# A two-layer perceptron by fast matrix products: more output buffers in chunk two, writes of x moved, and the first weight sums moved from GpSimd to VectorE and cut in halves

## The chip, the cores and the metric

The kernel runs on one core of a Trainium2 chip. TensorE (PE) multiplies matrices into PSUM (eight banks), VectorE (DVE) and ScalarE (ACT) read PSUM and SBUF, GpSimd (POOL) works on SBUF and issues transfers, SyncE (SP) only issues transfers. Each engine takes its own instructions in order, and semaphores tie them together. The metric is the time of one execution on the device in microseconds (us); lower is better. Several executions are timed, and one more is run under the hardware profiler.

## The reference

```python
batch, m, k, h, n = 16, 512, 768, 3072, 768      # x, w1, b1, w2 in float32
y = np.maximum(np.matmul(x, w1) + b1, 0)
return np.matmul(y, w2).astype(np.float32)
```

So 8192 rows of x go through a layer of 3072 hidden units and back to 768 columns.

## The kernel before, in words

Rows and hidden units are tiled so that both layers can be done with fewer products than blocks. Eight blocks of 1024 rows times two halves ("chunks") of the hidden units make 16 iterations: iterations 0 to 7 are chunk one, 8 to 15 chunk two. `NSB` is 8, `NIT` 16. Chunk one writes its output rows to DRAM, chunk two adds to them with accumulating transfers.

**First products (L475 to L589).** An iteration takes its rows of x as a 2 by 2 scheme of blocks, and each of its six strips of w1 (`TP` = 6) likewise. Iteration 0 uses plain products (`first_plain`, eight block products per strip, 24 matmuls of 512 columns). From iteration 1 on, `first` uses seven products per strip instead of eight, of 3 matmuls each, on sums of blocks: sums of x (`sums_x`, L383, slots `XS1`, `XS2`, `XS4` of the tile `x`) and sums of w1 (`sums_w1`, L281, slots `T1` to `T4` of a strip; `T3` takes the place of `B12`). ScalarE and VectorE turn the PSUM results into y; `s` is a scratch tile in SBUF with six slots, which first and second products share.

**Second products (L592 to L641).** y and w2 are combined in 20 products instead of the plain scheme's larger number, from sums of blocks of y (`sums_y`, L456, eight per pair of strips, on VectorE) and of w2 (`sum_w2`, L324, 16 sums, 15 of them on VectorE, the last one a negation on ScalarE). The list `SECOND` says for each of the 20 steps which product runs, into which pair of PSUM banks (q0 to q3), and which copies and sums follow it on ScalarE and VectorE. Eight of these are outputs o0 to o7, each 128 by 768 floats, made in the order o2, o3, o0, o5, o7, o4, o1, o6. Each takes a tile from a pool of four (L615) and is sent to DRAM at once: by SyncE in chunk one (L631), by GpSimd with accumulation in chunk two (L633).

**Order.** The program is written out by hand. `run` (L677) sorts the steps of all iterations by a key, so that the first strip of an iteration overlaps the last steps of the second products before it. After each step it pops one or two waiting sums of y (`fill`) and then runs the hooks that `plan` (L735) put behind it. A hook is named by kind, iteration, strip and step: `p1` plain first products, `m1` first products, `m2` second products. A step's place in this order is its place in the in-order stream of whichever engine or queue it uses, so an instruction that must wait holds up all that stands behind it on its engine.

What the diff touches:

- The loads at the start (L681 to L690) all stand in GpSimd's queue: strips of w1, twelve pieces of w2 (three for each of four slices s), rows of x.
- The sums of w1 for iteration 0 are hooks (L752 to L755): three for each strip after its first products, the fourth after step 4 of the second products, all 24 on GpSimd. The same function makes the sums for chunk two ahead of time (`ahead_w1`, L288).
- The sums of w2 for iteration 0 (L756 to L761) each take a whole block of 1536 columns: eight while strip 4 runs, one in strip 5, seven within the second products. Those for chunk two (L798 to L807) run at the end of iteration 7 and in iteration 8, from blocks fetched to the side into tiles of the pool `raw` and into x (`fetch_w2_aside`, L314).
- The second of the three sums of x (L392) runs on GpSimd.
- `save_x` (L400) writes x and its sums to DRAM for chunk two, in two parts, on SyncE's queue; for iterations 1 to 7 both are hooked behind step 16 of the second products before (L774, L775). `fetch_x` (L406) reads them back (L777, L779, L784).
- The pool `raw` has two buffers, for rows of x in chunk one and for w2 fetched aside in iterations 7 and 8.

Of the kernel before, what the change touches and what calls it, by code (L numbers as in the profile page):

```python
# [9 lines left out]
FP32 = mybir.dt.float32  # L10
# [3 lines left out]
ALU = mybir.AluOpType  # L14
# [135 lines left out]
class Fast:  # L150
# [127 lines left out]
                out=w[:, 2 * half:2 * half + 2].rearrange("p a k h -> p (a k) h"),  # L278
                in_=w1r[:, :, h0:h0 + P])

    def sums_w1(self, w, which=(0, 1, 2, 3)):  # L281
        every = ((self.T1, self.B12, self.B11), (self.T2, self.B22, self.T1),
                 (self.T4, self.B21, self.T2), (self.T3, self.B12, self.B22))
        for o, i, j in [every[n] for n in which]:
            self.nc.gpsimd.tensor_tensor(out=w[:, o], in0=w[:, i], in1=w[:, j],  # L285
                                         op=ALU.subtract)

    def ahead_w1(self, it, t, step):  # L288


        x0 = 4 * (it % 2)
        w = self.x[:, x0:x0 + 4].rearrange("p a k m -> p (a k m)")[:, 0:7 * 3 * P]
        w = w.rearrange("p (a k h) -> p a k h", a=7, k=3)
        if step == 0:
            self.load_strip(w, 1, t)
        elif step == 1:
            self.sums_w1(w)
        else:
            self.nc.sync.dma_start(out=self.w1dram[t], in_=w)

# [20 lines left out]
        self.nc.sync.dma_start(out=w, in_=self.w2dram[:, 2 * q:2 * q + 2])  # L321
        self.w2_raw[2 * q], self.w2_raw[2 * q + 1] = w[:, 0], w[:, 1]

    def sum_w2(self, n):  # L324

        o, i, j, sign = SUMS_W[n]

        def block(slot):
            return self.w2_raw.get(slot, self.v[:, slot].rearrange("p s n -> p (s n)"))

        out = self.v[:, o].rearrange("p s n -> p (s n)")
        if i is None:
            self.nc.scalar.activation(out=out, in_=block(j), func=ACTF.Copy,
                                      scale=float(sign))
        else:
            self.nc.vector.tensor_tensor(out=out, in0=block(i), in1=block(j),  # L336
                                         op=ALU.add if sign > 0 else ALU.subtract)
# [45 lines left out]
    def sums_x(self, it, which):  # L383

        x = self.x.rearrange("p a k m -> p a (k m)")
        a11 = 4 * (it % 2)
        a12, a21, a22 = a11 + 1, a11 + 2, a11 + 3
        if which == 0:
            self.nc.vector.tensor_tensor(out=x[:, self.XS1], in0=x[:, a21], in1=x[:, a22],  # L389
                                         op=ALU.add)  # L390
        elif which == 1:
            self.nc.gpsimd.tensor_tensor(  # L392
                out=x[:, a21:self.XS2 + 1:self.XS2 - a21],
                in0=x[:, a21:self.XS1 + 1:self.XS1 - a21],
                in1=x[:, a11:a11 + 1].to_broadcast((P, 2, 3 * self.MH)), op=ALU.subtract)
        else:
            self.nc.vector.tensor_tensor(out=x[:, self.XS4], in0=x[:, a12],
                                         in1=x[:, self.XS2], op=ALU.subtract)
# [193 lines left out]
    def second(self, it):  # L592
# [14 lines left out]
        def at(name):  # L607
# [2 lines left out]
                return self.ps[:, 2 * q:2 * q + 2, 0:NH]  # L610
            return self.s[:, int(name[1])].rearrange("p (a n) -> p a n", a=2)

        def total(engine, to, q, sign, kept=None, kept_sign=None):
            ps = at(f"q{q}")
            o = self.o_pool.tile([P, 2, NH], FP32, name="o") if to[0] == "o" else at(to)  # L615
            if kept is None:
                if engine == "ACT":
                    nc.scalar.activation(out=o, in_=ps, func=ACTF.Copy, scale=float(sign))  # L618
                else:
                    nc.vector.tensor_scalar(out=o, in0=ps, scalar1=float(sign), scalar2=None,  # L620
                                            op0=ALU.mult)
            else:
                a, b = (ps, at(kept)) if sign > 0 else (at(kept), ps)
                nc.vector.tensor_tensor(out=o, in0=a, in1=b,  # L624
                                        op=ALU.add if sign == kept_sign else ALU.subtract)
            if to[0] == "o":
                r, n = divmod(int(to[1]), 2)
                rows = self.of[row0 + r * QM:row0 + (r + 1) * QM, n * NH:(n + 1) * NH]
                rows = rows.rearrange("(j p) n -> p j n", p=P)
                if it < self.NSB:  # L630
                    nc.sync.dma_start(out=rows, in_=o)  # L631
                else:
                    nc.gpsimd.dma_start(out=rows, in_=o, accum_op=ALU.add)  # L633
# [43 lines left out]
    def run(self):  # L677
# [4 lines left out]
        self.constants()  # L682
        self.load_w1(1)
        self.load_x(0, (1,))
        for t in range(2, TP):
            self.load_w1(t)
        for s in range(4):
            for q in range(3):
                self.load_w2(self.v[:, 2 * q:2 * q + 2], 0, q, s)
        self.load_x(1, (0,))  # L690
# [44 lines left out]
    def plan(self):  # L735

        TP, NSB, NIT = self.TP, self.NSB, self.NIT
        self.hooks = {}

        def put(kind, it, q, i, fn, *args):  # L740
            self.hooks.setdefault((kind, it, q, i), []).append(lambda: fn(*args))
# [7 lines left out]
        put("p1", 0, 4, 1, self.transpose_x, 1, 0)  # L749
        put("p1", 0, 5, 1, self.transpose_x, 1, 1)  # L750
        put("m2", 0, 0, 3, self.save_x, 0, 0)
        for t in range(TP):  # L752
            put("p1", 0, max(t, 2), 3, lambda t: self.sums_w1(self.w1s[t], (0, 1, 2)), t)
        for t in range(TP):
            put("m2", 0, 0, 4, lambda t: self.sums_w1(self.w1s[t], (3,)), t)  # L755
        for n in range(8):  # L756
            put("p1", 0, 4, n // 2, self.sum_w2, n)
        for n, at in ((9, ("p1", 0, 5, 2)), (8, ("m2", 0, 0, 2)), (12, ("m2", 0, 0, 4)),
                      (10, ("m2", 0, 0, 5)), (14, ("m2", 0, 0, 7)), (13, ("m2", 0, 0, 9)),
                      (11, ("m2", 0, 0, 11)), (15, ("m2", 0, 0, 12))):  # L760
            put(*at, self.sum_w2, n)  # L761

        for it in range(NIT):
            nxt = it + 1
            if nxt < NSB:
# [5 lines left out]
                if nxt + 1 < NSB:  # L771
                    put("m2", it, 0, 5, self.load_x, nxt + 1, (0,))
                    put("m2", it, 0, 9, self.load_x, nxt + 1, (1,))
                put("m2", it, 0, 16, self.save_x, nxt, 0)  # L774
                put("m2", it, 0, 16, self.save_x, nxt, 1)  # L775
            elif nxt == NSB + 1:
                put("m2", it, 0, 8, self.fetch_x, nxt, 0)  # L777
            elif nxt < NIT:
                put("m1", it, 0, 4, self.fetch_x, nxt, 0)  # L779
            if nxt <= NSB:  # L780
                for n, i in enumerate((6, 7, 14)):
                    put("m2", it, 0, i, self.sums_x, nxt, n)
# [16 lines left out]
        put("m2", last, 0, 13, self.fetch_w2, B2)  # L799
        for n, at in ((2, ("m2", last, 0, 12)), (6, ("m2", last, 0, 14)),  # L800
                      (1, ("m2", last, 0, 16)), (15, ("m2", last, 0, 17)),
                      (3, ("m1", NSB, 0, 3)), (9, ("m1", NSB, 1, 1)), (7, ("m1", NSB, 1, 2)),
                      (0, ("m1", NSB, 1, 3)), (8, ("m1", NSB, 2, 1)), (5, ("m1", NSB, 2, 3)),
                      (12, ("m1", NSB, 3, 1)), (10, ("m2", NSB, 0, 5)),
                      (14, ("m2", NSB, 0, 6)), (4, ("m2", NSB, 0, 7)),
                      (13, ("m2", NSB, 0, 11)), (11, ("m2", NSB, 0, 14))):
            put(*at, self.sum_w2, n)  # L807

# [60 lines left out]
```

## Time and profile before

| What | us |
|---|---|
| Median of three runs | 933.2 (929.87 to 934.0) |
| Profiled execution, its own time | 931.92 |
| Span of that execution on the core | 930.4 |
| TensorE busy with matmuls | 875.0 (94%) |
| VectorE busy | 630.7 (68%) |
| ScalarE busy | 519.0 (56%) |
| GpSimd busy | 224.8 (24%) |

The page of the profile gives the busy time of each engine, then groups of instructions by line of the kernel: engine, operation, output and input by the program's names, shapes, how many, busy time, mean duration, and the idle time just before them with what ended it. `PEld` is the weight load of TensorE. The timeline has rows of start, length, engine, line and operation, several like instructions in a row merged (x8), with the idle time before them and its releaser in square brackets. Durations of instructions that follow one another closely overlap a little in the record, so the pitch in a row is shorter than a single duration.

### The profile page before, as it was taken

Reading aid. Unit: us, or ns where it says so; the run is one execution under the profiler, and the core shown is the slowest. Engines: PE = TensorE matmul, PEld = TensorE weight load, DVE = VectorE, ACT = ScalarE, POOL = GpSimd, SP = SyncE. Lnnn points to the kernel's source line nnn. Section 1 sums busy time; section 2 is a strip of 40 time slices with the busy share of each in tenths; the row PEclk is TensorE's granted clock in tenths of the full one; section 3 lists DMA queues with packets and bytes.
Section 4 is the critical chain, followed back from the end, with each engine's and each line's share of the span. In section 5 each row is a group of like instructions: output and inputs, shape, how many; then the busy total and the mean of one; then the engine's idle time right before and its main releaser. Section 6 shows DMA issues by size and latency. Waiting matters only on the chain.

```text
span 930.4 us, 12569 instructions
## 1 busy us (share of the span) xinstructions
PE 875.0 (94%) x4677; PEld 459.9 (49%) x4677; DVE 630.7 (68%) x1041; ACT 519.0 (56%) x791; POOL 224.8 (24%) x198
## 2 busy tenths in 40 slices
PE   8948999999999999999999899999999999999993
PEld 5424454554545555454545445455454545545452
DVE  2798676857767686776798656675766668566663
ACT  4723676757767576676346386675626345262530
POOL 6863042150503214040200301203030130402113
PEclk9978999999999999999999999999999999999997
DMA  9938849698687869818631925639173573815518
GB/s 201 199 110 162 254 86 309 87 248 209 133 283 108 294 86 265 173 70 343 270 119 51 228 45 153 102 119 136 36 156 64 145 110 119 122 19 101 83 18 120
DMA packets 120325, 138.11 MB, mean 148 GB/s; under 512 B 67116, under 2 KB 113732, under 8 KB 116420
## 3 DMA queue, kind: packets, MB, share of 16 engines
q0 software_dynamic: 50672, 46.41, 35.1%
q1 hardware_dynamic: 69264, 90.06, 29.7%
q10 hardware_dynamic: 324, 0.80, 0.3%
q8 instruction: 38, 0.62, 0.3%
q14 instruction: 27, 0.22, 0.1%
HBM read 72.17 MB, written 77.66 MB: 161 GB/s over the span
## 4 chain that ended last, share of the span: by engine, by line
PE 42%; issue 36%; DVE 8%; POOL 7%; DMA 4%; ACT 2%; POOLq 0%; DVEq 0%; ACTq 0%
PE ps L534 22%; PE ps L602 18%; POOL out_dram L633 7%; DMA out_dram<-o 4%; DVE o L624 2%; DVE v L336 2%; DVE y L466 2%; DVE ps L624 1%; DMA w1s<-in_w_dram 1%; PE ps L484 1%; ACT s L618 1%; ACT s L542 0%; ACT scrap L380 0%; ACT y L489 0%; DVE x L439 0%
## 5 line engine op out<-in xcount | busy, mean ns | idle before, releaser
L602 PE MATMUL ps<-v,y 128*128 128x384 f16 x2560 | 430.6, 329 | 17.3 <-DVE v L336 7.5
L534 PE MATMUL ps<-x,w1s 128*128 128x512 f16 x1890 | 417.0, 379 | 20.3 <-ACT s L542 14.2
L602 PEld LDWEIGHTS <-y 128*128 128x128 f16 x2560 | 251.4, 99 | 193.6 <-issue 11.0
L534 PEld LDWEIGHTS <-w1s 128*128 128x128 f16 x1890 | 184.9, 98 | 241.6 <-issue 25.2
L466 DVE TENSOR_TENSOR y<-y 128x512 f16<-128x512 f16 x512 | 212.0, 440 | 41.7 <-ACT y L551 26.3
L542 ACT ACTIVATE s<-ps,b1y 128x512 f32<-128x512 f32 x210 | 141.6, 687 | 172.1 <-PE ps L534 61.0
L546 DVE CUSTOM_DVE_ANT_0 y<-ps,s 128x512 f16<-128x512 f32 x210 | 144.9, 690 | 106.2 <-PE ps L534 73.6
L633 POOL DMA_DIRECT2D out_dram<-o x64 | 77.4, 1250 | 380.5 <-DVE o L624 378.5
L618 ACT ACTIVATE s<-ps 128x768 f32<-128x768 f32 x96 | 77.7, 810 | 133.4 <-PE ps L602 105.9
L624 DVE TENSOR_TENSOR o<-s,ps 128x768 f32<-128x768 f32 x64 | 61.0, 953 | 65.5 <-PE ps L602 22.7
L624 DVE TENSOR_TENSOR s<-ps,s 128x768 f32<-128x768 f32 x96 | 90.2, 953 | 12.6 <-ACT s L618 6.5
L624 DVE TENSOR_TENSOR o<-ps,s 128x768 f32<-128x768 f32 x64 | 59.3, 954 | 46.2 <-ACT s L618 36.4
L551 ACT ACTIVATE y<-ps,b1y 128x512 f16<-128x512 f32 x90 | 61.9, 687 | 39.7 <-PE ps L534 39.7
L392 POOL TENSOR_TENSOR x<-x 128x3072 f16<-128x3072 f16 x8 | 48.0, 6004 | 71.4 <-DVE x L389 71.4
L380 ACT ACTIVATE scrap<-xn 128x768 f16<-128x768 f16 x60 | 50.3, 838 | 0.8
L277 POOL DMA_DIRECT2D x<-in_w_dram x12 | 10.1, 848 | 163.7 <-PE ps L534 163.7
L557 ACT ACTIVATE ps<-ps,b1y 128x512 f32<-128x512 f32 x60 | 39.6, 659 | 10.8 <-PE ps L534 7.9
L551 ACT ACTIVATE y<-ps 128x512 f16<-128x512 f32 x60 | 35.8, 597 | 0.0
L344 ACT ACTIVATE scrap<-scrap 128x1536 f16<-128x1536 f16 x24 | 35.4, 1476 | 0.1
L618 ACT ACTIVATE ps<-ps 128x768 f32<-128x768 f32 x32 | 25.5, 798 | 9.8 <-PE ps L602 9.8
L484 PE MATMUL ps<-x,w1s 128*128 128x512 f16 x132 | 28.8, 379 | 0.4 <-DVE x L439 0.2
L285 POOL TENSOR_TENSOR w1s<-w1s 128x384 f16<-128x384 f16 x24 | 28.4, 1200 | 1.0
(64 smaller groups left out, 271.2 us busy)
## 6 DMA issues: line engine op xcount, KB each, us to landing
out_dram<-o SPq DMA_DIRECT2D x64, 384.0 KB, 5.2
out_dram<-o POOLq DMA_DIRECT2D x64, 384.0 KB, 6.3
xd<-x SPq DMA_DIRECT2D x8, 1536.0 KB, 6.5
x<-xd SPq DMA_DIRECT2D x8, 1536.0 KB, 8.2
xn<-in_x_dram POOLq DMA_DIRECT2D x15, 768.0 KB, 7.2
xd<-x SPq DMA_DIRECT2D x7, 1152.0 KB, 8.8
x<-xd SPq DMA_DIRECT2D x7, 1152.0 KB, 5.3
w1d<-x SPq DMA_DIRECT2D x6, 672.0 KB, 10.8
```

The lines of the kernel that those rows point to most:

```text
L380: self.nc.scalar.activation(out=self.junk(self.K), in_=rows, func=ACTF.Square, accum_out=self.stat[:, i:i + 1])
L392: self.nc.gpsimd.tensor_tensor(out=x[:, a21:self.XS2 + 1:self.XS2 - a21], in0=x[:, a21:self.XS1 + 1:self.XS1 - a21], in1=x[:, a11:a11 + 1] ...
L466: self.nc.vector.tensor_tensor(out=pair(*outs), in0=pair(*ins0), in1=pair(*ins1), op=ALU.add if sign > 0 else ALU.subtract)
L534: nc.tensor.matmul(ps, lhsT=w[:, slot, k, :], rhs=x[:, xslot, k, :], start=(start and k == 0), stop=(k == 2), skip_group_check=True)
L542: nc.scalar.activation(out=kept(name), in_=ps, func=ACTF.Identity, bias=bias)
L546: nc.vector._custom_dve(TENSOR_ADD_SAT, out=self.y_of(self.TP * half + t, m), in0=self.two(ps), in1=self.two(kept(name)), s0=F_MAX, s1=0.0)
L551: nc.scalar.activation(out=self.y_of(self.TP * half + t, m), in_=self.two(ps), func=ACTF.Relu, **kw)
L557: nc.scalar.activation(out=g["b"], in_=g["a"], func=ACTF.Identity, bias=bias1)
L602: nc.tensor.matmul(self.ps[:, 2 * q + j, 0:NH], lhsT=self.y[:, U_OF[p], m0:m0 + P], rhs=self.v[:, V_OF[p], s, :], start=(start and s == 0) ...
L618: nc.scalar.activation(out=o, in_=ps, func=ACTF.Copy, scale=float(sign))
L624: nc.vector.tensor_tensor(out=o, in0=a, in1=b, op=ALU.add if sign == kept_sign else ALU.subtract)
L633: nc.gpsimd.dma_start(out=rows, in_=o, accum_op=ALU.add)
```

## The change

Four things change.

- In chunk two from iteration 9 on, the outputs o5 and o7 share one tile from the pool `raw`, half each, and so do o1 and o6. The pool of four is left to o2, o3, o0 and o4.
- The two DRAM writes of x and its sums move from step 16 of the second products into the first products of the next iteration, the sums behind step 0 of strip 1 and x behind step 0 of strip 4. Fetches of x in chunk two move to other places too.
- In iteration 0 the 24 sums of w1 run on VectorE; three per strip come within the first products, the fourth one strip at a time in steps 8 to 13 of the second products. The sums of w2 are made as two halves each (slices 0 and 1, then 2 and 3), the first halves during strips 2 and 3, the second halves from strip 4 on, five of them within the second products. The loads of w1 strips and of w2 slices alternate. The second sum of x for iteration 1 also goes to VectorE.
- Some sums of w2 for chunk two move: sums 9 and 7 to steps 17 and 18 of iteration 7's second products, sum 4 from iteration 8's second products to its first. Sums 10 and 14 there read block B2 from its own slot instead of the copy aside.

```diff
-    def sums_w1(self, w, which=(0, 1, 2, 3)):
+    def sums_w1(self, w, engine, which=(0, 1, 2, 3)):
...
-            self.nc.gpsimd.tensor_tensor(out=w[:, o], in0=w[:, i], in1=w[:, j],
-                                         op=ALU.subtract)
+            engine.tensor_tensor(out=w[:, o], in0=w[:, i], in1=w[:, j], op=ALU.subtract)
...
-    def sum_w2(self, n):
+    def sum_w2(self, n, s0=0, s1=4):
 
         o, i, j, sign = SUMS_W[n]
 
-        def block(slot):
-            return self.w2_raw.get(slot, self.v[:, slot].rearrange("p s n -> p (s n)"))
-
-        out = self.v[:, o].rearrange("p s n -> p (s n)")
+        def block(slot, raw=self.w2_raw):
+            w = raw.get(slot, self.v[:, slot].rearrange("p s n -> p (s n)"))
+            return w[:, s0 * self.NH:s1 * self.NH]
+
+        out = block(o, {})
+        if self.w2_raw and o in (V6, V14):
+            self.w2_raw.pop(B2, None)
...
-            self.nc.gpsimd.tensor_tensor(
+            (self.nc.gpsimd if it > 1 else self.nc.vector).tensor_tensor(
...
+        pairs = {}
+
+        def output(to):
+
+            pair = {"o5": 0, "o7": 0, "o1": 1, "o6": 1}.get(to)
+            if it <= self.NSB or pair is None:
+                return self.o_pool.tile([P, 2, NH], FP32, name="o")
+            if pair not in pairs:
+                pairs[pair] = [self.raw_pool.tile([P, 4, NH], FP32, name="o2", tag="raw"), 0]
+            half = pairs[pair][1]
+            pairs[pair][1] = 2
+            return pairs[pair][0][:, half:half + 2]
+
...
-            o = self.o_pool.tile([P, 2, NH], FP32, name="o") if to[0] == "o" else at(to)
+            o = output(to) if to[0] == "o" else at(to)
...
-        for t in range(2, TP):
-            self.load_w1(t)
         for s in range(4):
+            self.load_w1(2 + s)
             for q in range(3):
                 self.load_w2(self.v[:, 2 * q:2 * q + 2], 0, q, s)
...
+        for t, at in enumerate(((1, 1), (1, 2), (2, 0), (2, 2), (3, 1), (4, 0))):
+            put("p1", 0, *at, lambda t: self.sums_w1(self.w1s[t], vector, (0, 1, 2)), t)
         for t in range(TP):
-            put("p1", 0, max(t, 2), 3, lambda t: self.sums_w1(self.w1s[t], (0, 1, 2)), t)
-        for t in range(TP):
-            put("m2", 0, 0, 4, lambda t: self.sums_w1(self.w1s[t], (3,)), t)
-        for n in range(8):
-            put("p1", 0, 4, n // 2, self.sum_w2, n)
-        for n, at in ((9, ("p1", 0, 5, 2)), (8, ("m2", 0, 0, 2)), (12, ("m2", 0, 0, 4)),
-                      (10, ("m2", 0, 0, 5)), (14, ("m2", 0, 0, 7)), (13, ("m2", 0, 0, 9)),
-                      (11, ("m2", 0, 0, 11)), (15, ("m2", 0, 0, 12))):
-            put(*at, self.sum_w2, n)
+            put("m2", 0, 0, 8 + t, lambda t: self.sums_w1(self.w1s[t], vector, (3,)), t)
+        for n in range(15):
+            put("p1", 0, 2 + n // 8, n % 8 // 2, self.sum_w2, n, 0, 2)
+            late = {10: 3, 12: 4, 14: 5, 13: 6, 11: 7}.get(n)
+            at = ("m2", 0, 0, late) if late else ("p1", 0, 4 + (n + 2) // 8, (n + 2) % 8 // 2)
+            put(*at, self.sum_w2, n, 2, 4)
+        put("m2", 0, 0, 12, self.sum_w2, 15)
...
-                put("m2", it, 0, 16, self.save_x, nxt, 0)
-                put("m2", it, 0, 16, self.save_x, nxt, 1)
-            elif nxt == NSB + 1:
-                put("m2", it, 0, 8, self.fetch_x, nxt, 0)
+                put("m1", nxt, 1, 0, self.save_x, nxt, 1)
+                put("m1", nxt, 4, 0, self.save_x, nxt, 0)
             elif nxt < NIT:
-                put("m1", it, 0, 4, self.fetch_x, nxt, 0)
+                put("m1", it, 4 if nxt == NSB + 1 else 2, 4, self.fetch_x, nxt, 0)
...
-                      (3, ("m1", NSB, 0, 3)), (9, ("m1", NSB, 1, 1)), (7, ("m1", NSB, 1, 2)),
-                      (0, ("m1", NSB, 1, 3)), (8, ("m1", NSB, 2, 1)), (5, ("m1", NSB, 2, 3)),
-                      (12, ("m1", NSB, 3, 1)), (10, ("m2", NSB, 0, 5)),
-                      (14, ("m2", NSB, 0, 6)), (4, ("m2", NSB, 0, 7)),
+                      (9, ("m2", last, 0, 17)), (7, ("m2", last, 0, 18)),
+                      (3, ("m1", NSB, 0, 3)), (0, ("m1", NSB, 1, 1)), (8, ("m1", NSB, 1, 2)),
+                      (4, ("m1", NSB, 1, 3)), (5, ("m1", NSB, 2, 1)), (12, ("m1", NSB, 2, 3)),
+                      (10, ("m2", NSB, 0, 5)), (14, ("m2", NSB, 0, 6)),
```

More of the change, by code (lines that the diff above doesn't have):

```diff
@@ L296, in ahead_w1 @@
         elif step == 1:
-            self.sums_w1(w)
+            self.sums_w1(w, self.nc.gpsimd)
         else:
@@ L738, in plan @@
         self.hooks = {}
+        vector = self.nc.vector
         def put(kind, it, q, i, fn, *args):
```

## The prediction

> **What bounds the kernel now.** I read the busy table first, then the stages side by side (one stage per iteration, cut where its last product begins), then the timeline of TensorE for its gaps, then VectorE and GpSimd around each gap.
>
> ```profile
> span 930.4 us, 12569 instructions
> PE 875.0 (94%) x4677; PEld 459.9 (49%) x4677; DVE 630.7 (68%) x1041; ACT 519.0 (56%) x791; POOL 224.8 (24%) x198
> ...
> 44.14:94.37 50.23, 33.18 (x164) 17.76 (x165) 46.65 (x46) 16.05 (x27) 26.68 (x20) 0.80 0.63 147
> ...
> 366.04:419.61 53.57, 53.38 (x288) 27.92 (x286) 37.48 (x64) 35.65 (x56) 11.26 (x7) 1.00 0.61 160
> ```
>
> TensorE is the bound: an undisturbed iteration (366.04 to 419.61) takes 53.57 us and TensorE works through all but 0.2 of it. (After the stretch and its length a stage's row has the busy time of TensorE, its weight loads, VectorE, ScalarE and GpSimd, then clock, DMA share and GB/s.) So only time in which it waits can be won, and that lies in four places. The first is the second half of iteration 0 (second row): 33.18 us of work in 50.23 us, at a granted clock of 0.80.
>
> ```profile
> 418.47 1.30 PE ps L602 x8
> 419.77 25.25 PE ps L534 x117
> ...
> 18.08 26.06 PE L484 MATMUL ps<-x,w1s 128*128 128x512 f16 x120 [0.24 <-DVE x L439]
> 53.08 4.15 PE L602 MATMUL ps<-v,y 128*128 128x384 f16 x14 [6.95 <-DVE v L336]
> 63.20 15.26 PE L602 MATMUL ps<-v,y 128*128 128x384 f16 x82 [5.97 <-DVE y L466]
> 82.07 10.51 PE L602 MATMUL ps<-v,y 128*128 128x384 f16 x48 [3.61 <-DVE o L624]
> ```
>
> At full speed eight matmuls of L602 take 1.30 us (0.162 each) and one of L534 25.25/117 = 0.216. That stretch holds 160 of the one and 3 of the other, so 26.6 us where 50.2 pass: 23.6 lost, 16.5 of it as the three gaps of the last rows, before which VectorE is late, the rest as small waits and slower matmuls behind them. VectorE is late because of GpSimd:
>
> ```profile
> L285 POOL TENSOR_TENSOR w1s<-w1s 128x384 f16<-128x384 f16 x24 | 28.4, 1200 | 1.0
> L466 DVE TENSOR_TENSOR y<-y 128x512 f16<-128x512 f16 x15 | 16.2, 1112 | 2.6 <-ACT y L489 2.4
> ...
> L466 DVE TENSOR_TENSOR y<-y x4: 410/411/413, 62.4 to 63.4; 128x512 f16<-128x512 f16 x4
> 510.92 1.82 DVE L336 TENSOR_TENSOR v<-w2r,x 128x1536 f16<-128x1536 f16 x2
> 74.17 6.99 DVE L336 TENSOR_TENSOR v<-v 128x1536 f16<-128x1536 f16 x2
> ```
>
> The first two rows are groups between 32.3 and 60.9 us, while GpSimd makes its 24 sums of w1: a sum of y takes 1.11 us. Just after, the same sum takes 0.41. Two sums of w2 alone take 1.82 together (0.95 each, 0.87 apart); beside GpSimd's 6 us sum of x (last row) two take 6.99.
>
> The other places are the ends of iterations:
>
> ```profile
> 151.49 22.82 PE L534 MATMUL ps<-x,w1s 128*128 128x512 f16 x105 [0.80 <-DMA out_dram<-o]
> 206.10 22.82 PE L534 MATMUL ps<-x,w1s 128*128 128x512 f16 x105 [0.89 <-ACT s L542]
> 261.49 22.82 PE L534 MATMUL ps<-x,w1s 128*128 128x512 f16 x105 [1.66 <-ACT s L542]
> 528.72 0.81 PE L534 MATMUL ps<-x,w1s 128*128 128x512 f16 x3 [2.99 <-DVE o L624]
> 535.92 22.82 PE L534 MATMUL ps<-x,w1s 128*128 128x512 f16 x105 [2.50 <-ACT s L542]
> ...
> L534 PE MATMUL ps<-x,w1s 128*128 128x512 f16 x879 | 194.1, 379 | 11.6 <-ACT s L542 11.6
> ```
>
> The last row is the group of L534 from 531 us to the end: 11.6 us of waits for ScalarE, so 9.1 beside the 2.50 at 535.92, one wait at the end of each of iterations 9 to 14 (1.5 each).
>
> **The change, part by part.**
>
> *w1 and w2 sums of iteration 0.* GpSimd loses all 24 sums and one 6 us sum of x. VectorE gains them: a 384-wide sum by the slope between 512 (0.41) and 1536 (0.95) is 0.34 alone, 0.27 in a row; the sum of x, twice 1536, 1.7; and w2 comes as halves of 768, 0.55 alone, 0.47 in a row. From 24.0 us (strip 1 ends at 18.08+24x0.217 = 23.3, ScalarE needs 0.7) VectorE has until the end of first products: 24 sums of y at 0.36 (0.41 alone, overlapping), 12 of w1 at 0.27, 25 halves at 0.47: 8.6+3.2+11.8 = 23.6, so it ends at about 48, TensorE at 44.1. Data is there:
>
> ```profile
> 22.88 2.81 DVE L466 TENSOR_TENSOR y<-y 128x512 f16<-128x512 f16 x7 [4.52 <-ACT y L489]
> ...
> 24.37 0.70 POOL L307 DMA_DIRECT2D v<-in_w_dram  x1 [0.44 <-DMA w1s<-in_w_dram]
> ...
> 29.35 0.71 POOL L307 DMA_DIRECT2D v<-in_w_dram  x1 [0.25 <-DMA v<-in_w_dram]
> v<-in_w_dram POOLq DMA_DIRECT2D x1, 192.0 KB, 7.6
> ```
>
> The last load of w2 is issued at 29.35 and lands 7.6 later, at 37.0, about one load per us; the new order moves the same bytes, so the last strip of w1 lands near 33 (strip 5 begins at 18.08+96x0.217 = 38.9) and the first half of w2 near 26, where VectorE wants it at 26.5. In the second products VectorE has 4 us of lag and 5 halves, 6 sums of w1 and the sum of x more: 2.4+1.6+1.7 = 5.7. What covers it is its own idle time in such a stage:
>
> ```profile
> 353.60 0.95 DVE L624 TENSOR_TENSOR o<-s,ps 128x768 f32<-128x768 f32 x1 [2.72 <-ACT ps L618]
> 358.29 0.96 DVE L624 TENSOR_TENSOR o<-ps,s 128x768 f32<-128x768 f32 x1 [2.42 <-ACT s L618]
> 366.24 0.95 DVE L624 TENSOR_TENSOR o<-s,ps 128x768 f32<-128x768 f32 x1 [0.47 <-PE ps L602]
> ```
>
> That is 5.6 of the 9.7; uncovered, up to 4 us reach TensorE, and 2 more if the last outputs meet loads. The early products read finished halves, so some lag is free: I take 2.5 left of the 23.6, bounds 0.5 and 6: **21.1 won** (17.6 to 23.1).
>
> One rule of the Trainium skill must be weighed, since the loads are issued on GpSimd while VectorE now works without a pause. In the trace the load of w2 issued at 24.37 lies beside seven sums of y (22.88 to 25.69) and takes 0.70 us, the one at 29.35 with VectorE all but idle 0.71. SBUF — State Buffer, section "SBUF: two separate sides", describes one exclusive port pair for both engines: a two-input VectorE operation excludes a GpSimd one that reads SBUF (the rows above agree: 1.11 against 0.41), and a VectorE operation in a two-port mode starves the writing of DMA descriptors as well; "A bandwidth-pool intuition that's wrong" gives 620 ns against 3100 for such a DMA. If the second half held for these sums, the saving would shrink; the fourth rival gives it as a mechanism.
>
> *Writes of x.* Each pair (1536 and 1152 KB) leaves the queue of SyncE from between the fifth and sixth output and goes behind the outputs, around the next transposes.
>
> ```profile
> 149.10 0.96 DVE L624 TENSOR_TENSOR o<-s,ps 128x768 f32<-128x768 f32 x1 [1.43 <-DMA out_dram<-o]
> 146.52 0.85 SPq L404 DMA_DIRECT2D xd<-x  x2
> ...
> w2d<-in_w_dram POOLq DMA_DIRECT2D x3, 192.0 KB, 6.8
> out_dram<-o SPq DMA_DIRECT2D x1, 384.0 KB, 5.8
> ```
>
> The eighth output waits for the buffer of the fourth, which takes 5.8 us to land, so was issued near 143.3; three loads of w2 run then too, and the writes of x come only from 146.52. Iterations 4 to 6 have the same writes and no stall, so the loads may be the cause. Bounds: 0 and the whole 0.80+0.89+1.66 = 3.35. I take the middle, **1.7**. Moved past: transposes for the next iteration, with some 20 us to spare.
>
> *Output buffers of chunk two.*
>
> ```profile
> 588.46 0.95 DVE L624 TENSOR_TENSOR o<-s,ps 128x768 f32<-128x768 f32 x1 [1.82 <-DMA out_dram<-o]
> ...
> DMA  0000958971999500979999999999999998410000
> ```
>
> From iteration 9 on, the eighth output waits for a buffer (first row, iteration 9); it also holds the s that ScalarE overwrites, and TensorE waits for that. Eight buffers remove the wait; without it the last output starts when TensorE's last product allows (366.24 above) and 117 matmuls run without a gap. **9.1 won**; bounds 7 and 9.1. At the very end the last output can leave up to 1.8 earlier, but the last row (busy tenths of the DMA engines, 900 to 930.4 us in 40 slices) shows the accumulating DMAs at work without a gap from 913 to 926, so I take 0.5 (0 to 1.8).
>
> *Iteration 8* keeps four buffers.
>
> ```profile
> 527.71 0.96 DVE L624 TENSOR_TENSOR o<-ps,s 128x768 f32<-128x768 f32 x1 [2.84 <-DMA out_dram<-o]
> ...
> x<-xd SPq DMA_DIRECT2D x2, 1536.0 KB, 9.5
> out_dram<-o POOLq DMA_DIRECT2D x1, 384.0 KB, 13.7
> ...
> out_dram<-o POOLq DMA_DIRECT2D x1, 384.0 KB, 5.2
> ```
>
> The buffer that its fifth output waits for is the first's, which takes 13.7 us to land beside two fetches of x (second row); in iteration 9 the first takes 5.2 (last row). The fetch for iteration 9 now waits for no late sum of w2, so both run before the first output: the stall falls from 5.49 to the 1.5 to 1.75 of its neighbours: **3.75 won** (0 to 4.5).
>
> *Two sums of w2 into the end of iteration 7*, between the last three outputs.
>
> ```profile
> 471.94 0.95 DVE L336 TENSOR_TENSOR v<-w2r 128x1536 f16<-128x1536 f16 x1
> ...
> 474.53 0.95 DVE L624 TENSOR_TENSOR o<-s,ps 128x768 f32<-128x768 f32 x1
> ```
>
> Each (0.87 in a row) stands ahead of an output on VectorE. ScalarE and then TensorE wait for the last one, and it has no slack: **1.75 lost** (0 to 2).
>
> **Sum.** 21.1+1.7+9.1+0.5+3.75-1.75 = 34.4 us off the profiled execution's 931.92 us (its span 930.4 and 1.5 around it): 897.5. That execution lies 1.3 under the median of the runs, 933.2, so I forecast **898**.
>
> **Rivals.**
> 1. *VectorE becomes the bound of iteration 0*: sums cost 0.55 rather than 0.47, 40 times 0.08 = 3 more, and its idle time covers nothing because products come late too. Then 4+3+5.7 = 12.7 of the 23.6 remain and 10.9 are won: 897.5+10.2 = 908. For it: 23.6 us of work in 20. Against: 5.6 us of cover.
> 2. *The wait in chunk two moves on*: a later output waits for GpSimd's issues or for the bank, and half or all of the 9.1 stays: 903 to 907. Against: 366.24.
> 3. *The stalls at 528 and 535 stay and the writes of x give nothing* (3.75+1.7): 903.
> 4. *VectorE holds up the loads*: an issue of 0.70 that has to wait for two half sums (0.94) takes 1.64 where a load lands about every 1.03 now; 20 loads then end 12 us later, the second halves with them, and some 10 of the 21.1 are gone: 908. Against: 0.70 at 24.37. By the figures of the skill's page on SBUF the loads would end 41 us later (20 times 3.1 less 1.03) and nearly the whole gain would be lost; no row here shows such an issue.
> 5. *Slower*: the two outputs that share one tile are held apart as a whole, not by halves. Then the second half of each pair waits until the first has landed: 5.2 us (iteration 9, above) plus its own sum of 1, less the 1 to 2 by which it follows anyway, 4.5 each and 9 an iteration where 1.5 are lost now. From 9 to 15: 7x7.5 = 52, less the other 25.3 won: 959. It decides from 1.5+25.3/7 = 5.1 us of wait an iteration. Against: `ps`, `v` and `x` are single tiles whose parts are written and read side by side in all rows above.
>
> **How the numbers follow.** The forecast as summed, 890 to 902: 0.63. Rivals 1 and 2: 0.14 and 0.08, 3: 0.07, two of these together (912 to 917): 0.03, all of 1 to 4 (931): 0.01. Rival 4 alone: 0.01, rival 5: 0.02; better than 890: 0.01. Range 888 to 909, from all 3.35 and 23.1 won down to rival 1. Within 0.5% (4.7 us, what a measurement here can tell from no change) only the four together lie: faster 0.97, same 0.01, slower 0.02.
>
> **What would show it.** Right: sums of y near 0.4 and halves near 0.55 from 24 us on; second products from 44.1 to some 73 at a clock near 1.00; iterations 10 to 15 at 53.4 us; no wait of an output for a DMA there; first output of iteration 8 landing in under 6. Wrong: issues of loads above 1 us, gaps of TensorE before 44 us, gaps over 1 us at the ends of iterations 9 to 14, or an output landing that the second half of a pair waits for.

## The result, and the profile after

The changed kernel takes 901.9 us (median of four runs, 901.39 to 903.64), beside 933.6 (929.87 to 935.03) for the kernel before on the same chip: a ratio of 0.967, interval 0.9639 to 0.9701. The forecast was 898, range 888 to 909. The profiled execution took 901.8 us where that of before took 931.92, so 30.1 us went, of 34.4 forecast. New lines shift the numbers: L534 is now L536, L602 is L604, L542 is L544, L466 is L468, L336 is L338, L624 is L639.

Span and busy table of the page after, answering to the first lines shown of before:

```profile
span 900.2 us, 12564 instructions
PE 868.4 (96%) x4677; PEld 458.1 (51%) x4677; DVE 618.4 (69%) x1081; ACT 519.5 (58%) x791; POOL 190.9 (21%) x173
```

TensorE does the same 4677 matmuls and remains the bound. GpSimd is busy 34 us less. VectorE has 40 instructions more and is busy 12 us less, since much of its time before was spent held up inside its instructions.

The stages after (stretch, length, busy TensorE, weight loads, VectorE, ScalarE, GpSimd, then clock, DMA share, GB/s): second products of iteration 0, then iterations 1, 8, 9, 10 as cut in the prediction.

```profile
44.17:73.84 29.67, 27.19 (x163) 15.74 (x162) 27.70 (x48) 16.07 (x27) 3.51 (x5) 1.00 1.02 223
73.84:129.56 55.72, 53.53 (x288) 27.89 (x286) 38.34 (x65) 35.53 (x56) 14.82 (x12) 1.00 0.74 177
...
456.23:511.81 55.58, 53.52 (x288) 27.89 (x286) 46.28 (x75) 33.11 (x44) 6.53 (x6) 1.00 0.47 127
511.81:566.60 54.79, 53.50 (x289) 28.04 (x287) 35.84 (x62) 36.99 (x52) 10.12 (x10) 1.00 0.53 108
566.60:620.00 53.40, 53.40 (x289) 28.04 (x287) 36.06 (x63) 37.10 (x52) 9.93 (x10) 1.00 0.54 112
```

The first row was 50.23 at a clock of 0.80 and is 29.67 at 1.00: 20.56 won, 3 us above its floor of 26.6. The second stage took 53.57 before and takes 2.15 more. Iterations 8 and 9 together fall by 2.13; iteration 10 runs without a pause.

The gaps of TensorE after, in its timeline: within the second products of iteration 0 (first row), then at the ends of iterations.

```profile
49.95 10.90 PE L604 MATMUL ps<-v,y 128*128 128x384 f16 x66 [1.89 <-DVE y L468]
...
78.60 22.82 PE L536 MATMUL ps<-x,w1s 128*128 128x512 f16 x105 [2.00 <-ACT s L544]
133.51 22.82 PE L536 MATMUL ps<-x,w1s 128*128 128x512 f16 x105 [1.18 <-ACT s L544]
188.04 22.82 PE L536 MATMUL ps<-x,w1s 128*128 128x512 f16 x105 [0.80 <-ACT s L544]
243.37 22.82 PE L536 MATMUL ps<-x,w1s 128*128 128x512 f16 x105 [1.60 <-ACT s L544]
...
460.88 22.82 PE L536 MATMUL ps<-x,w1s 128*128 128x512 f16 x105 [1.88 <-ACT s L544]
515.86 22.82 PE L536 MATMUL ps<-x,w1s 128*128 128x512 f16 x105 [1.29 <-ACT s L544]
```

Of the gaps of 6.95, 5.97 and 3.61 us in the second products one of 1.89 is left. The gap at 78.60 is new, the three behind it stand nearly as they were (0.80, 0.89 and 1.66 before), the 1.88 at 460.88 is new, and after 515.86 there is none. The group of L536 from 511.8 us to the end says the same of chunk two, where it had 11.6 us of waits:

```profile
L536 PE MATMUL ps<-x,w1s 128*128 128x512 f16 x879 | 193.1, 379 | 1.3 <-ACT s L544 1.3
```

On VectorE between 18 and 74 us (groups: count, busy, mean ns, idle before) the sums have their undisturbed lengths, and w1 (L285) is a small item:

```profile
L338 DVE TENSOR_TENSOR v<-v 128x768 f16<-128x768 f16 x30 | 15.5, 553 | 1.6 <-DMA w1s<-in_w_dram 1.5
L468 DVE TENSOR_TENSOR y<-y 128x512 f16<-128x512 f16 x32 | 12.6, 421 | 2.7 <-ACT y L491 2.4
L285 DVE TENSOR_TENSOR w1s<-w1s 128x384 f16<-128x384 f16 x24 | 8.3, 356 | 0.4
```

### The profile page after: what moved, and what is told of

Same layout as the page of the kernel before. It is cut to its first block, busy times and chain, and to the rows that moved or that the text cites. A ratio compares the mean times of both kernels' runs of the same rounds, so it can differ in the third digit from the quotient of the medians.

```text
span 900.2 us, 12564 instructions
## 1 busy us (share of the span) xinstructions
PE 868.4 (96%) x4677; PEld 458.1 (51%) x4677; DVE 618.4 (69%) x1081; ACT 519.5 (58%) x791; POOL 190.9 (21%) x173
## 4 chain that ended last, share of the span: by engine, by line
PE 40%; issue 36%; POOL 9%; DVE 6%; DMA 6%; ACT 2%; POOLq 0%; DVEq 0%; ACTq 0%
PE ps L536 23%; PE ps L604 18%; POOL out_dram L648 8%; DMA out_dram<-o 3%; DVE o L639 3%; DMA v<-in_w_dram 2%; DVE ps L639 1%; DVE v L338 1%; DMA w1s<-in_w_dram 1%; ACT s L633 1%; ACT s L544 1%; POOL w1s L277 1%; DVE y L468 0%; DVE w1s L285 0%; DVE x L391 0%
## 5 line engine op out<-in xcount | busy, mean ns | idle before, releaser
L536 PE MATMUL ps<-x,w1s 128*128 128x512 f16 x1890 | 416.2, 379 | 11.7 <-ACT s L544 8.8
L604 PE MATMUL ps<-v,y 128*128 128x384 f16 x2560 | 424.6, 326 | 2.5 <-DVE y L468 1.9
L604 PEld LDWEIGHTS <-y 128*128 128x128 f16 x2560 | 249.5, 98 | 174.4 <-ACT y L553 2.5
L536 PEld LDWEIGHTS <-w1s 128*128 128x128 f16 x1890 | 184.8, 98 | 232.4 <-issue 15.4
L544 ACT ACTIVATE s<-ps,b1y 128x512 f32<-128x512 f32 x210 | 142.0, 687 | 162.4 <-DVE y L548 53.9
L468 DVE TENSOR_TENSOR y<-y 128x512 f16<-128x512 f16 x512 | 201.8, 420 | 32.9 <-ACT y L553 25.6
L639 DVE TENSOR_TENSOR o<-s,ps 128x768 f32<-128x768 f32 x64 | 61.0, 953 | 60.1 <-PE ps L604 26.7
L639 DVE TENSOR_TENSOR s<-ps,s 128x768 f32<-128x768 f32 x96 | 90.2, 954 | 12.5 <-ACT s L633 6.5
L639 DVE TENSOR_TENSOR o<-ps,s 128x768 f32<-128x768 f32 x64 | 58.8, 953 | 36.8 <-ACT s L633 34.9
L394 POOL TENSOR_TENSOR x<-x 128x3072 f16<-128x3072 f16 x7 | 42.1, 6009 | 65.7 <-DVE x L391 53.1
L369 POOL DMA_DIRECT2D xn<-in_x_dram x15 | 11.5, 764 | 74.3 <-ACT scrap L382 73.5
```

Source lines behind the costliest of these rows:

```text
L394: (self.nc.gpsimd if it > 1 else self.nc.vector).tensor_tensor(out=x[:, a21:self.XS2 + 1:self.XS2 - a21], in0=x[:, a21:self.XS1 + 1:self.X ...
L468: self.nc.vector.tensor_tensor(out=pair(*outs), in0=pair(*ins0), in1=pair(*ins1), op=ALU.add if sign > 0 else ALU.subtract)
L536: nc.tensor.matmul(ps, lhsT=w[:, slot, k, :], rhs=x[:, xslot, k, :], start=(start and k == 0), stop=(k == 2), skip_group_check=True)
L544: nc.scalar.activation(out=kept(name), in_=ps, func=ACTF.Identity, bias=bias)
L604: nc.tensor.matmul(self.ps[:, 2 * q + j, 0:NH], lhsT=self.y[:, U_OF[p], m0:m0 + P], rhs=self.v[:, V_OF[p], s, :], start=(start and s == 0) ...
L639: nc.vector.tensor_tensor(out=o, in0=a, in1=b, op=ALU.add if sign == kept_sign else ALU.subtract)
```

## The experiments

Each starts from the changed kernel, except one, which starts from the kernel before and says so in its title. "After" is 901.9 throughout. The runs of the kernel before that were made beside the experiments have medians of 932.1 to 932.9, where those beside after had 933.6, and the ratios are against the former. So a difference from after of 1.5 us or less between medians tells nothing.

### Four output buffers in chunk two again

```diff
-            if it <= self.NSB or pair is None:
+            if True:
```

> The changed kernel, but all eight outputs of chunk two take the four buffers as before. My theory: the eighth output waits for the landing of the fourth again, six gaps of 1.2 to 1.9 us come back before L536 at the ends of iterations 9 to 14, and the time is some 10 us longer than the changed kernel's 901.9: 911 to 912. Rival (the fetches of x, which also moved, were what made the landings late): no gaps, within 2 us of 901.9.

Measured: 914.27 us (913.13 to 916.57), ratio 0.9807 (0.9784 to 0.983), 12.4 more than after. The timeline of TensorE in this kernel, first of iteration 0, then of iterations 9 to 14:

```profile
79.35 24.51 PE L536 MATMUL ps<-x,w1s 128*128 128x512 f16 x105 [2.49 <-ACT s L544]
...
573.54 22.82 PE L536 MATMUL ps<-x,w1s 128*128 128x512 f16 x105 [1.31 <-ACT s L544]
628.28 22.82 PE L536 MATMUL ps<-x,w1s 128*128 128x512 f16 x105 [1.39 <-ACT s L544]
683.86 22.82 PE L536 MATMUL ps<-x,w1s 128*128 128x512 f16 x105 [1.79 <-ACT s L544]
738.95 22.82 PE L536 MATMUL ps<-x,w1s 128*128 128x512 f16 x105 [1.33 <-ACT s L544]
794.24 22.82 PE L536 MATMUL ps<-x,w1s 128*128 128x512 f16 x105 [1.94 <-ACT s L544]
848.96 22.82 PE L536 MATMUL ps<-x,w1s 128*128 128x512 f16 x105 [1.37 <-ACT s L544]
```

All six stalls are back, 9.13 us in sum, with nothing else of chunk two changed: the buffers remove them and make no new wait. The time lies above the 911 to 912 expected. From iteration 10 on the profiled execution is 10.6 us longer than that of after: a stall costs some 0.15 more than its gap (117 matmuls without a break take 25.42 us, 12 and 105 with a gap between them 2.75 and 22.82), and its last stretch, to the end of the span, is 0.5 longer. It also lost 2.2 at the end of iteration 0, where the gap was 0.5 longer and the 105 matmuls behind it took 24.51 instead of 22.82 (the last section comes back to that), and 1.0 in a gap behind iteration 4.

### Writes of x back behind step 16

```diff
-                put("m1", nxt, 1, 0, self.save_x, nxt, 1)
-                put("m1", nxt, 4, 0, self.save_x, nxt, 0)
+                put("m2", it, 0, 16, self.save_x, nxt, 0)
+                put("m2", it, 0, 16, self.save_x, nxt, 1)
```

> The changed kernel with the writes of x back behind step 16 of the second products. Theory after the result: these writes were never what the outputs waited for, so gaps at the ends of iterations 1 to 3 stay at 0.8 to 1.6 us and the time within 1.5 us of 901.9. Rival (my prediction's: they delay the landings by half of it): 1.7 to 3.5 us longer, gaps above 1.5 us each.

Measured: 903.25 us (900.79 to 906.06), ratio 0.9692 (0.9671 to 0.9713). Its gaps at the ends of iterations 0 to 3 in TensorE's timeline:

```profile
78.01 22.82 PE L536 MATMUL ps<-x,w1s 128*128 128x512 f16 x105 [1.48 <-ACT s L544]
132.84 22.82 PE L536 MATMUL ps<-x,w1s 128*128 128x512 f16 x105 [1.10 <-ACT s L544]
187.23 22.82 PE L536 MATMUL ps<-x,w1s 128*128 128x512 f16 x105 [0.66 <-ACT s L544]
242.65 22.82 PE L536 MATMUL ps<-x,w1s 128*128 128x512 f16 x105 [1.69 <-ACT s L544]
```

Beside 2.00, 1.18, 0.80 and 1.60 after, three are shorter and one is 0.09 longer. The 1.35 between the medians is less than the spread of these runs, so no effect of the writes is seen, and the prediction's 1.7 for them falls. Another cause was named there: the loads of w2.

### The loads of w2 for chunk two, moved behind the outputs

```diff
-            put("m1", 1 + n // 3, 3 + n % 3, 0, self.load_w2,
+            put("m2", 1 + n // 3, 0, 2, self.load_w2,
```

> The changed kernel with the twelve loads of w2 for chunk two (iterations 1 to 4, GpSimd's queue) put behind step 2 of the second products, where that queue waits for TensorE to be done with x. Theory (these loads make the fourth output land late): landings of outputs fall below 5 us, the gaps of 1.18, 0.80 and 1.60 us at the ends of iterations 1 to 3 go below 0.5 each, 2.5 to 4.5 us shorter, 898 to 899.5. Rival (the landing is set by the outputs themselves or the loads of rows of x): gaps and time stay, 901 to 902.5.

Measured: 895.81 us (895.13 to 896.22), ratio 0.9607 (0.9582 to 0.9631), 6.1 less than after. First three views of the kernel after: GpSimd's timeline in iteration 1, the transfers of outputs between 120 and 190 us (count, KB each, median us from issue to landing), and VectorE's timeline at the ends of iterations 0 and 1.

```profile
124.17 2.07 POOL L306 DMA_DIRECT2D w2d<-in_w_dram  x3
...
out_dram<-o SPq DMA_DIRECT2D x14, 384.0 KB, 5.9
...
76.21 0.95 DVE L639 TENSOR_TENSOR o<-s,ps 128x768 f32<-128x768 f32 x1 [1.13 <-DMA out_dram<-o]
...
131.12 0.95 DVE L639 TENSOR_TENSOR o<-s,ps 128x768 f32<-128x768 f32 x1 [1.81 <-PE ps L536]
```

The same views of the experiment, where the loads have moved from 124.17 to 153.19 (behind a strip load that waits for TensorE), and a row of TensorE's timeline, at the end of iteration 0:

```profile
153.19 2.04 POOL L306 DMA_DIRECT2D w2d<-in_w_dram  x3
...
out_dram<-o SPq DMA_DIRECT2D x14, 384.0 KB, 3.0
...
127.78 0.95 DVE L639 TENSOR_TENSOR o<-s,ps 128x768 f32<-128x768 f32 x1 [0.47 <-PE ps L604]
...
74.01 25.42 PE L536 MATMUL ps<-x,w1s 128*128 128x512 f16 x117
```

The median landing is 3.0 us instead of 5.9, the last output of iteration 1 waits 0.47 instead of 1.81, and TensorE's gaps at the ends of iterations 0 to 3 are gone, the 2.00 of iteration 0 included (last row: 117 matmuls in one piece). The expectation had not counted that one, and so fell short. The row at 131.12 names a matmul as what came last, but the buffer came free just then: the sum that makes the fourth output of iteration 1 ends at 124.84, and its transfer takes 6.2 us to land, until some 131.0. With the loads moved that landing takes 4.0. At 76.21 the row names the landing itself. So the stalls at the ends of iterations 0 to 3 were outputs waiting for buffers, and their cause is the twelve loads (three an iteration) that ran beside the output writes.

### The sums of w1 on GpSimd, at the new places

```diff
-    ... self.sums_w1(self.w1s[t], vector, (0, 1, 2)), t)
+    ... self.sums_w1(self.w1s[t], self.nc.gpsimd, (0, 1, 2)), t)
...
-    ... self.sums_w1(self.w1s[t], vector, (3,)), t)
+    ... self.sums_w1(self.w1s[t], self.nc.gpsimd, (3,)), t)
```

> The changed kernel with the 24 sums of w1 of iteration 0 on GpSimd, all else as changed (halves, order of loads, places). Theory (GpSimd's two-input sums hold VectorE's up): sums of y beside them take 1.0 us or more instead of 0.42, half sums of w2 1.0 instead of 0.55, the second products of iteration 0 take 38 us or more instead of 29.7, time 910 to 922. Rival (the gain came from the earlier start of the w2 sums): durations stay, 901 to 904.

Measured: 913.77 us (912.86 to 916.16), ratio 0.981 (0.9789 to 0.9831), 11.9 more than after. Its groups between 18 and 75 us:

```profile
L338 DVE TENSOR_TENSOR v<-v 128x768 f16<-128x768 f16 x30 | 27.5, 952 | 2.8 <-DMA v<-in_w_dram 2.8
L285 POOL TENSOR_TENSOR w1s<-w1s 128x384 f16<-128x384 f16 x24 | 24.2, 1022 | 1.0
L468 DVE TENSOR_TENSOR y<-y 128x512 f16<-128x512 f16 x32 | 18.7, 610 | 4.8 <-ACT y L491 4.5
```

and its timelines of VectorE (first two rows) and TensorE:

```profile
38.41 2.18 DVE L468 TENSOR_TENSOR y<-y 128x512 f16<-128x512 f16 x2
40.52 2.44 DVE L338 TENSOR_TENSOR v<-v 128x768 f16<-128x768 f16 x2
...
53.93 2.72 PE L604 MATMUL ps<-v,y 128*128 128x384 f16 x8 [9.09 <-DVE v L338]
```

With 24 sums of some 1 us on GpSimd, the 30 halves cost VectorE 27.5 us instead of 15.5 and the sums of y 18.7 instead of 12.6. VectorE is late by more than the 8.3 us it saves, TensorE waits 9.09 in one piece, and the second products take 44.32 us instead of 29.67. The place of the sums is not what helps; their engine is.

### The kernel before with the sums of w1 on VectorE, at the old places

```diff
-            put("p1", 0, max(t, 2), 3, lambda t: self.sums_w1(self.w1s[t], (0, 1, 2)), t)
+            put("p1", 0, max(t, 2), 3, lambda t: self.sums_w1(self.w1s[t], (0, 1, 2), True), t)
...
-            put("m2", 0, 0, 4, lambda t: self.sums_w1(self.w1s[t], (3,)), t)
+            put("m2", 0, 0, 4, lambda t: self.sums_w1(self.w1s[t], (3,), True), t)
```

> The kernel before with one edit: its 24 sums of w1 of iteration 0 on VectorE at the old places, with whole sums of w2, the old order of loads and the 6 us sum of x on GpSimd. Theory (which engine is most of it): sums of y near 0.42, second products of iteration 0 in 34 to 38 us instead of 50.2, time 917 to 922 against 933.6. Rival (placement is most of it): 928 or more.

Measured: 922.54 us (921.95 to 924.26), ratio 0.9902 (0.9883 to 0.9921), 9.9 less than before, so the rival is out. The sums of y take 0.42, as expected, but the time lies just above the expected range and the stage of second products takes 40.68 us, more than the 34 to 38 that I expected. Its timelines of VectorE and TensorE show why:

```profile
65.21 6.98 DVE L336 TENSOR_TENSOR v<-v 128x1536 f16<-128x1536 f16 x2
...
73.11 9.36 PE L602 MATMUL ps<-v,y 128*128 128x384 f16 x48 [4.12 <-DVE o L624]
```

The 6 us sum of x is still on GpSimd and holds two sums of w2 for 6.98. The expectation names that sum but puts no price on it.

### The sum of x back on GpSimd

```diff
-            (self.nc.gpsimd if it > 1 else self.nc.vector).tensor_tensor(
+            self.nc.gpsimd.tensor_tensor(
```

> The changed kernel with the second sum of x for iteration 1 back on GpSimd (6 us). Theory: VectorE's sums of two SBUF operands beside it wait for its end (one operation of several us, as the two in 6.99 us before), TensorE gets a gap of 2 us or more in the second products of iteration 0, time 904 to 908. Rival: VectorE is relieved by 1.7 us and nothing is lost: 900 to 902.

Measured: 904.64 us (903.49 to 906.9), ratio 0.9706 (0.968 to 0.9733), 2.7 more than after. Its timelines of GpSimd, VectorE and TensorE:

```profile
59.28 5.99 POOL L394 TENSOR_TENSOR x<-x 128x3072 f16<-128x3072 f16 x1 [3.64 <-DVE x L391]
59.97 5.71 DVE L338 TENSOR_TENSOR v<-v 128x768 f16<-128x768 f16 x1
67.14 10.88 PE L604 MATMUL ps<-v,y 128*128 128x384 f16 x48 [3.38 <-DVE o L639]
```

One half sum that takes 0.55 alone takes 5.71 and ends 0.4 us after GpSimd's instruction, and TensorE waits 3.38. On VectorE the same sum of x takes 1.75. The second products take 33.75, 4.1 more than after, but the gap of 2.00 behind them doesn't come, so the 2.7 us is a net price.

### Whole sums of w2, and the old order of loads

Whole sums at the places of the second halves:

```diff
-            put("p1", 0, 2 + n // 8, n % 8 // 2, self.sum_w2, n, 0, 2)
...
-            put(*at, self.sum_w2, n, 2, 4)
+            put(*at, self.sum_w2, n)
```

> The changed kernel without the early halves: each sum of w2 of iteration 0 made whole at the place of its second half, all sums still on VectorE. Theory (the halves spread the work over a time in which VectorE idles): VectorE idles from 27 to 36 us and is later by 4 to 7 us afterwards, second products of iteration 0 33 to 37 us instead of 29.7, time 905 to 909. Rival (the engine was all of it): 901 to 903.

Measured: 901.07 us (900.19 to 903.93), ratio 0.9668 (0.9647 to 0.9688): no difference from after. My theory fell and the rival held. The 15 whole sums, all at strip 4 and later, take 13.8 us where the halves take 15.5, and the second products take 30.96 where the halves give 29.67. VectorE's idle time earlier, which the halves were to fill, was small: two waits of 3.7 us in sum between 27.8 and 32.0. And the 1.29 that the halves win in the second products goes again behind them, where the gap is 2.00 after and 0.84 here. Whether the halves pay once the loads of w2 are moved was not tried.

All strips of w1 loaded first again, with the halves kept:

```diff
+        for t in range(2, TP):
+            self.load_w1(t)
         for s in range(4):
-            self.load_w1(2 + s)
```

> The changed kernel with the old order of loads: all strips of w1, then all of w2. Theory: the first halves of w2 land 4 us later (30 instead of 26), VectorE stands waiting for them and is late by some 3 us more, part of it absorbed: 903 to 906. Rival (no effect, the wait is hidden): 901 to 902.5.

Measured: 905.77 us (904.74 to 908.23), ratio 0.9716 (0.9695 to 0.9737), 3.9 more than after. VectorE's timeline shows the price of halves without their data:

```profile
30.76 1.03 DVE L338 TENSOR_TENSOR v<-v 128x768 f16<-128x768 f16 x2 [5.78 <-DMA v<-in_w_dram]
```

The new order of loads is needed by the early halves. Whole sums with the old order were not tried, so what the order alone is worth stays open.

### Sums 9 and 7 into the first products of iteration 8, alone and with the later loads

```diff
-                      (9, ("m2", last, 0, 17)), (7, ("m2", last, 0, 18)),
-                      (3, ("m1", NSB, 0, 3)), (0, ("m1", NSB, 1, 1)), (8, ("m1", NSB, 1, 2)),
+                      (3, ("m1", NSB, 0, 3)), (9, ("m1", NSB, 0, 5)), (7, ("m1", NSB, 0, 6)),
+                      (0, ("m1", NSB, 1, 1)), (8, ("m1", NSB, 1, 2)),
```

> The changed kernel with sums 9 and 7 of w2 put from between the last outputs of iteration 7 into strip 0 of iteration 8's first products. Theory: the gap of 1.88 us in iteration 8's first strip goes below 0.5, time 1.5 to 1.9 us shorter, about 900.2. Rival: VectorE is late within those first products instead and as much is lost there: 901.5 to 902.5.

Measured: 901.95 us (901.25 to 903.88), ratio 0.9678 (0.9652 to 0.9703): nothing won in the median. Its timeline of TensorE:

```profile
78.67 24.51 PE L536 MATMUL ps<-x,w1s 128*128 128x512 f16 x105 [2.09 <-ACT s L544]
...
468.44 15.70 PE L536 MATMUL ps<-x,w1s 128*128 128x512 f16 x72 [0.55 <-DVE y L548]
```

The 1.88 at 460.88 is gone, but the two sums now stand ahead of the y of the first strips and a wait of 0.55 comes back; what this execution kept at iteration 8, about 1 us, it lost in slower matmuls behind 78.67 (24.51 us instead of 22.82). So I put the two sums behind strips 3 and 4 of iteration 8, together with the later loads:

```diff
-            put("m1", 1 + n // 3, 3 + n % 3, 0, self.load_w2,
+            put("m2", 1 + n // 3, 0, 2, self.load_w2,
...
-                      (9, ("m2", last, 0, 17)), (7, ("m2", last, 0, 18)),
+                      (9, ("m1", NSB, 3, 2)), (7, ("m1", NSB, 4, 2)),
```

> The changed kernel with the loads of w2 later, as in the run that did this alone (895.8), and sums 9 and 7 of w2 taken from between the last outputs of iteration 7 to strips 3 and 4 of iteration 8's first products, where VectorE has pauses. Theory: the gap of 1.88 us in iteration 8's first strip goes and no new one comes, 893.5 to 894.5. Rival (VectorE late elsewhere, as in the run that put them into strip 0, which won nothing): 895 to 896.5.

Measured: 895.12 us (893.37 to 896.47), ratio 0.9594 (0.9577 to 0.9611). The stage of iteration 8, in this kernel:

```profile
448.32:502.17 53.85, 53.52 (x287) 27.89 (x287) 46.15 (x76) 33.22 (x44) 4.85 (x4) 1.00 0.47 133
```

and with the later loads alone:

```profile
448.53:504.11 55.58, 53.52 (x287) 27.92 (x287) 46.45 (x76) 33.10 (x44) 4.85 (x4) 1.00 0.45 129
```

In the profiled executions 1.73 us are gone from the stage, as the theory has it. But the median lies above the 893.5 to 894.5 expected and inside the rival's range, and the medians of the two kernels differ by 0.7, less than their spread, so the gain in time is not settled. With either of the two, the kernel is some 6 us faster than after and 37 faster than before.

## Why the prediction was right, and where it was not

**The sum.** 897.5 and the 1.3 by which the execution lay under the median make 898.8, so the working gives 899 where 898 stands. All of 3.35 and 23.1 won takes 897.5 to 893.9, so the lower end of 888 has no sum behind it. The measured 901.9 lies 0.1 inside the band of 890 to 902 and as near to the 903 of rival 3, so the number alone could not have told them apart, and half of rival 3 came true (the writes); the traces tell.

**Iteration 0 (21.1 won by the prediction).** 20.56 in its stage, by the step as forecast: sums of y at 0.42 and halves at 0.55, clock 1.00, the stage 29.67 long where some 29 were forecast. But 2.15 of that comes back at the start of iteration 1, as the new gap of 2.00 at 78.60, so 18.4 net, inside the bounds of 17.6 to 23.1. The step that failed is "I take 2.5 left": it foresaw "2 more if the last outputs meet loads" and then left it out. They do meet them: moving the loads took the gap away. So 5.2 of the 23.6 stayed, not 2.5. Why the stage shrinks is shown by four runs. GpSimd's two-input sums hold up VectorE's; the 24 sums of w1 on GpSimd are worth 11.9 us put back and 9.9 taken away alone, the sum of x 2.7, and the order of loads 3.9 once there are early halves. The halves themselves gave nothing here. These prices aren't additive, since each is what VectorE's lag leaves uncovered beside the others.

One rule of the Trainium skill fits the mechanism: SBUF — State Buffer, section "SBUF: two separate sides", has a VectorE operation with two SBUF inputs and a GpSimd operation that reads SBUF share one port pair as a lock, which the one that starts first holds for its whole instruction. The 5.71 us for a half sum that starts 0.69 us behind the 5.99 us sum of x agree with it.

**Writes of x (1.7 won).** Wrong: nothing. The gaps at the ends of iterations 1 to 3 went from 3.35 to 3.58 in sum, and putting the writes back changed none of them by more than 0.14. The step that failed is the choice of the middle between 0 and 3.35 although "the loads may be the cause" stood beside it with its evidence, the absence of stalls in iterations 4 to 6, which have the writes and not the loads.

**Output buffers of chunk two (9.1 won).** Right, with the size a little low: the stages from iteration 10 to the end took some 10.2 us less, worked out as the 30.1 less the differences of the stages ahead of it (20.56, -2.15, -0.6 for iterations 2 to 5, 2.13). The excess over 9.1 is mostly the break itself, which costs some 0.15 beside each gap; the four-buffer run gives 10.6 for the same stretch, 0.5 of it at its very end. No wait took the place of the old one (from iteration 10 on VectorE's L639 waits for TensorE and ScalarE alone), so rival 2 is out, and the outputs that share a tile don't hold each other, so rival 5 is out too: iteration 10 takes 53.40.

**The tail (0.5 won).** From the end of TensorE's last product to the end of the span passed 14.27 us before and 14.22 after: nothing, the lower bound.

**Iterations 7 and 8 (3.75 won, 1.75 lost).** 2.0 net forecast, 2.13 measured: the stall of 2.99 and 2.50 fell to a 1.29, and the lost 1.75 is the 1.88 at 460.88. Moving the two sums away removed that gap, which shows its cause. For the stall that fell, the two fetches of x are now issued at 485.71, ahead of the first output of iteration 8, and that output lands in 5.2 us where it took 13.7:

```profile
out_dram<-o POOLq DMA_DIRECT2D x1, 384.0 KB, 5.2
```

This fits the forecast, but no run puts the fetch back alone, so this cause is argued and not shown.

**VectorE as the bound, and late loads (rivals 1 and 4).** Neither came. Halves took 0.55 each as single instructions and overlapped in a row; the load issues beside them did not grow:

```profile
26.55 1.03 DVE L338 TENSOR_TENSOR v<-v 128x768 f16<-128x768 f16 x2 [1.50 <-DMA w1s<-in_w_dram]
...
26.65 0.70 POOL L306 DMA_DIRECT2D v<-in_w_dram  x1 [0.17 <-issue]
```

An issue in the middle of two half sums takes the same 0.70 as before, and so do all seven issues of this line after 17.9 us (0.70 or 0.71).

In sum, 34.4 forecast less 2.15 (the outputs that meet loads), 1.7 (writes), 0.5 (tail), 0.5 (iteration 0's stage) and 0.6 (small losses in iterations 2 to 5), plus 1.1 (chunk two) and 0.1 (iterations 7 and 8), is 30.15, beside 30.1 measured.

## What to carry to other kernels

A two-input sum on GpSimd cost VectorE most of its length where VectorE had such sums of its own waiting (18.1 of 24.2 us for the sums of w1, 5.2 of 6.0 for the sum of x): price it as time of both engines, and move it where VectorE does it in a third of the time (0.36 us against 1.02 for 384 columns here). Where an output waits for its buffer, look at what else is in flight while the buffer's transfer lands: moving twelve small loads out of the output phase was worth 6 us here. Where two causes are possible, ask first which iterations have one of them and no stall.

## What was unexpected of the hardware

**What is held and what isn't.** GpSimd's sum of x holds a half sum of w2, but VectorE's operations with an operand in PSUM keep their length: L639 takes 0.95 beside it. The changed kernel's timelines of GpSimd and VectorE in iteration 1:

```profile
113.69 6.01 POOL L394 TENSOR_TENSOR x<-x 128x3072 f16<-128x3072 f16 x1 [1.79 <-DVE x L391]
...
117.14 0.95 DVE L639 TENSOR_TENSOR o<-s,ps 128x768 f32<-128x768 f32 x1 [2.73 <-ACT ps L633]
```

The output at 117.14 runs within GpSimd's sum and is as long as those outside it.

**Loads and landings.** Three loads of 192 KB that GpSimd issues lengthen the landing of SyncE's outputs of 384 KB from 3.0 to 5.9 us, the medians of 14 outputs each, and that of the fourth output of iteration 1, on whose buffer the eighth waits, from 4.0 to 6.2.

**The granted clock after a gap.** Behind the gaps of 2.09 and 2.49 us at the end of iteration 0 (the rows at 78.67 and 79.35) the 105 matmuls took 24.51 us, behind one of 2.00 in the same place 22.82. The windows of the four-buffer kernel show the clock:

```profile
76.00:80.00 4.00, 1.51 (x7) 0.54 (x6) 1.55 (x2) 1.84 (x3) 0.00 (x0) 0.94 0.77 282
80.00:84.00 4.00, 4.00 (x13) 1.55 (x12) 1.38 (x2) 0.86 (x2) 0.00 (x0) 0.63 0.99 325
```

0.63 in the second stretch. A length is not the whole condition, since in the kernel before the clock stayed at 1.00 behind gaps of 2.99 and 2.50 (iteration 8), and the 105 matmuls took 22.82. In the same place, behind a gap of 3.03, it fell to 0.54 (519.5 to 522 us) in the kernel before with the sums of w1 on VectorE. TensorE: Matmul & The Clock Gate, in the Trainium skill, section "HAM oscillation — how this bites in real kernels", asks for no idle gap above about 3.4 us; here the clock fell after shorter ones. What decides it is open. It means that a small wait can cost more than its length, here 1.7 us on top.
